# FFN output projection of a hybrid transformer block: one product of float32 operands in place of three products of split parts

## The chip, the cores and the metric

The kernel runs on one core of a Trainium2 chip. The core has a matrix engine (TensorE, PE in the profile, with its loads of stationary operands listed apart as PEld), a vector engine (VectorE, DVE), a scalar engine (ScalarE, ACT), a general engine (GpSimd, POOL) and an engine that here issues most of the DMAs (SyncE, SP). Each engine works through its own queue of instructions in order and waits on semaphores for the others. The matrix engine takes a stationary operand (`lhsT`) and a moving operand (`rhs`) from SBUF and adds the product into a PSUM bank.

The metric is the time of one execution on the device in microseconds, as the median of several runs. A profile is one further execution with the hardware profiler on.

## The reference

The whole block has a mixer of three branches and then a feed-forward network. Only its last lines matter here: 512 tokens, `D_MODEL` 1024, `D_FF` 2816, everything in float32.

```python
    h = rms_norm(x, ffn_pre_g[l])
    gate, up = jnp.split(h @ w_ffn_in[l], 2, axis=-1)
    x = x + rms_norm((jax.nn.silu(gate) * up) @ w_ffn_out[l], ffn_post_g[l])
```

The changed product is `(silu(gate) * up) @ w_ffn_out`, a 512 x 2816 matrix times a 2816 x 1024 matrix.

## The kernel before

**The two kinds of operand.** The program marks a matrix operand either as plain `F32` or as `F32R`, which is four bytes in memory too. Where a dense product matters for accuracy, the kernel splits a float32 value `v` into two `F32R` parts: a high part `h`, written by ScalarE in a copy that rounds, and a low part `l = v - h`, written by VectorE. A product of two split operands is then three matrix instructions, high by high, high by low, low by high, added in the same PSUM bank. `mm3` issues them, and all the large projections of the kernel go through it. Its three instructions have lines 137, 138 and 139 in the profile:

```python
        first = mm(ps, lhsT=lh, rhs=rh, start=start, stop=False)
        mm(ps, lhsT=lh, rhs=rl, start=False, stop=False)
        return first, mm(ps, lhsT=ll, rhs=rh, start=False, stop=stop)
```

Smaller products elsewhere in the kernel take plain `F32` operands directly: in the attention heads line 1138 multiplies the transposed probabilities by the values (80 calls in the source: 8 heads of 1 + 2 + 3 + 4 tiles, each a 128 x 128 by 128 x 128 product), line 1001 multiplies squares by a column of ones, and line 843 forms 32 x 32 blocks of scores.

**Weights.** `slab` brings a piece of a weight matrix of 128 x 512 values (256 KB) from HBM into a staging tile `wsD` of the pool `wD`, splits it into `whD` and `wlD`, and returns both. Each of the three names has three buffers in rotation (`bufs=3`), unless the caller wants the split parts kept in a pool of its own:

```python
        st = self.t(self.wd, [P, m, n], "wsD", bufs=3)
        nc.sync.dma_start(st, src)
        h, l = (self.t(pool or self.wd, [P, m, n], t, F32R, hold or 3) for t in ("whD", "wlD"))
        nc.scalar.copy(h, st)
        self.split_low(l, st, h)
```

The DMA is issued by SP (line 201), the copy by ScalarE (line 205), the subtraction by VectorE (line 132, in `split_low`).

**The feed-forward network.** `ffn` first runs over the 22 row blocks of `w_ffn_in` in pairs (`stream`, at the PSUM tiles `mmD`). For each block, `up` multiplies gate and up part (line 1261), and then writes the result `t` halved and split: `fH` by ScalarE (line 1262) and `fL` by VectorE (line 1263). `fH` and `fL` are tiles of 128 x 22 x 512 values, 44 KB of each partition apiece, and live in the pool `ffn` with the buffers of the output projection.

Then `project` multiplies by `w_ffn_out`. It is also used once earlier, for `w_out` after the three branches, with the split operands `mH` and `mL`. The 1024 output columns are done in two halves (`n`), each with four PSUM banks `po0` to `po3`, one for each 128 tokens. Within a half the loop goes over the 22 blocks `k` of the contraction: one slab of weights, and for each of the four token tiles one product, 128 tokens of `x` as the stationary operand and the slab's 512 columns as the moving one (`part`). The second half does so for the first 16 slabs only; the last 6 (`hold`) are kept in the pool `ffn`, and the token tiles are finished one after the other over these six, so that the norm of one tile runs beside the products of the next. Behind each tile's last product come a sum of squares on ScalarE (line 1232), a multiplication by the gain on VectorE (line 1233), in the second half the reciprocal root on GpSimd (line 279), the addition to the residual (line 1286) and the store (line 1287). The residual `x1` is read back from HBM (line 1281) into tiles that held the FFN's input before.

**Order.** The program is written with a tile framework that inserts the waits. It orders instructions by a priority that rises along the program; `lane` moves parts of the program to other priorities, and `lane(0)` puts the weight splits ahead. A buffer of a rotating tile is given to its next user when its last reader is done.

Of the kernel before, what the change touches and what calls it, by code (L numbers as in the profile page):

```python
# [11 lines left out]
F32 = mybir.dt.float32  # L12
F32R = mybir.dt.float32r
# [3 lines left out]
AF = mybir.ActivationFunctionType  # L17
ALU = mybir.AluOpType
# [4 lines left out]
P = 128  # L23
S = 512
# [10 lines left out]
KF = DFF // P  # L35
# [67 lines left out]
class Kern:  # L103
# [92 lines left out]
    def slab(self, src, pool=None, hold=None):  # L196

        nc = self.nc
        m, n = src.shape[1:]
# [3 lines that stand above are left out]
        cur = self.cur_lane  # L203
        self.lane(0)
        nc.scalar.copy(h, st)  # L205
        self.split_low(l, st, h)
        self.lane(cur)
        return h, l
# [996 lines left out]
    def project(self, pool, pp, x, w, nk, gp, done, hold):  # L1205


        nc = self.nc
        V, A = nc.vector, nc.scalar
        w = w.rearrange("(k p) n -> p k n", p=P)  # L1210
        y = [self.t(pool, [P, D], f"y{i}") for i in range(NT)]
        ss = self.t(pool, [P, NT, 2], "pss")
        for n in range(2):
            c = slice(n * 512, (n + 1) * 512)
            ps = [self.t(pp, [P, 512], f"po{i}") for i in range(NT)]

            def part(i, k, wk):
                h, l = wk
                tok = slice(i * P, (i + 1) * P)
                self.mm3(ps[i], x[0][:, k, tok], x[1][:, k, tok], h[:, 0], l[:, 0], k == 0, k == nk - 1)  # L1220

            first = nk - hold * n
            for k in range(first):
                wk = self.slab(w[:, k:k + 1, c])
                for i in range(NT):
                    part(i, k, wk)
            held = [self.slab(w[:, k:k + 1, c], pool, hold) for k in range(first, nk)]
            for i in range(NT):
                for k in range(first, nk):
                    part(i, k, held[k - first])  # L1230
                junk = self.t(pool, [P, 512], "pjk", bufs=2)
                A.activation(junk, ps[i], AF.Square, accum_out=ss[:, i, n:n + 1])
                V.tensor_tensor(y[i][:, c], ps[i], gp[:, c], op=ALU.mult)
                if n:
                    s1, tm, rs = (self.t(pool, [P, 1], t, bufs=2) for t in ("rs1", "rtm", "rrs"))
                    V.tensor_tensor(s1, ss[:, i, 0:1], ss[:, i, 1:2], op=ALU.add)
                    self.rstd(rs, s1, D, NEPS, tm)
                    done(i, y[i], rs)

    def ffn(self, x1d):  # L1240
        nc, tc, ins = self.nc, self.tc, self.ins
        V, A = nc.vector, nc.scalar
        es = self.ctx
        fp = es.enter_context(tc.tile_pool(name="ffn", bufs=1))
        fH, fL = self.t(fp, [P, KF, S], "fH", F32R), self.t(fp, [P, KF, S], "fL", F32R)
        gp = self.t(fp, [P, D], "gp")
        nc.scalar.dma_start(gp, ins["ffn_post_g"][0:1, :].to_broadcast([P, D]))
        win = ins["w_ffn_in"][0].rearrange("(k p) n -> p k n", p=P)
        self.stream_psum(es, 4)
        po = es.enter_context(tc.tile_pool(name="pfo", bufs=1, space=PSUM))  # L1250
        for f in range(0, KF, 2):
            ts_ = [self.t(fp, [P, S], f"ft{j}", bufs=2) for j in range(2)]

            def gate(j, pg):
                t = ts_[j]
                A.activation(t, pg, AF.Tanh, scale=0.5)
                V.scalar_tensor_tensor(t, t, 1.0, pg, op0=ALU.add, op1=ALU.mult)

            def up(j, pu):
                t = ts_[j]  # L1260
                V.tensor_tensor(t, t, pu, op=ALU.mult)
                A.activation(fH[:, f + j], t, AF.Copy, scale=0.5)
                V.scalar_tensor_tensor(fL[:, f + j], t, 0.5, fH[:, f + j].bitcast(F32), op0=ALU.mult, op1=ALU.subtract)

            wg, wu = win[:, :, f * P:(f + 2) * P], win[:, :, DFF + f * P:DFF + (f + 2) * P]
            if f:
                self.stream(wg, self.h, gate)
                self.stream(wu, self.h, up)
            else:

                a, b = slice(0, S // 2), slice(S // 2, S)
                pg = self.stream(wg, self.h, None, a)
                pu = self.stream(wu, self.h, None, a)
                self.stream(wg, self.h, gate, b, pg)
                self.stream(wu, self.h, up, b, pu)


        x1 = [[self.t(self.hp, [P, 512], f"xH{2 * i + n}") for n in range(2)] for i in range(NT)]
        for i in range(NT):
            for n in range(2):  # L1280
                nc.sync.dma_start(x1[i][n], x1d[i][:, n * 512:(n + 1) * 512])

        def done(i, y, rs):
            for n in range(2):
                c = slice(n * 512, (n + 1) * 512)
                V.scalar_tensor_tensor(x1[i][n], y[:, c], rs, x1[i][n], op0=ALU.mult, op1=ALU.add)
                nc.sync.dma_start(self.out[0, i * P:(i + 1) * P, c], x1[i][n])

        self.project(fp, po, (fH, fL), ins["w_ffn_out"][0], KF, gp, done, 6)

    def run(self):
        self.full = True
# [73 lines left out]
```

## Time and profile before

| What | Value |
|---|---|
| median of 2 runs | 1406.16 us (1403.6 to 1408.73) |
| the profiled execution, on the same clock as the runs | 1408.42 us |
| its span, first to last instruction | 1406.6 us |
| mean granted TensorE clock | 0.996 of full speed |
| VectorE busy | 848.3 us (60%), 1756 instructions |
| ScalarE busy | 638.6 us (45%), 1259 instructions |
| HBM read and written | 169.65 MB and 60.16 MB |

A row of a group or tile gives the line in the program, the engine, the operation, the tiles as `out<-in`, the shape, the number of instructions and their durations. For a matrix instruction `128*128 128x512` means 128 contraction rows by 128 stationary columns, with 512 moving columns. The profile writes `f32` for matrix operands of either kind. Matrix instructions overlap: a duration of 389 ns says that one instruction is in the engine for so long, while the next starts much sooner, so the cost in a row of them is the distance between starts. Durations of waiting instructions are not in the busy time, but idle time before an instruction is listed with what ended it.

### The profile page before, as it was taken

The page shows a single profiled execution, that of the slowest core. Times are in us where ns is not written, and L with a number is a line of the kernel's source. Part 1 is how long each engine was busy: PE and PEld are TensorE (multiplying, and loading weights), DVE is VectorE, ACT ScalarE, POOL GpSimd, SP SyncE. Part 2 cuts the span into 40 slices and gives each one's busy share as a digit, 9 for nine tenths or more (in the row PEclk, how much of TensorE's full clock was granted, in tenths as well). Part 3 has the DMA queues.
Part 4 walks back from the last instruction along what each step waited for, and adds up shares of the span by engine and source line. Part 5 has one row for each costly group of instructions (what it writes and reads, how often), then busy time and mean ns, then how long its engine had stood idle before and what let it go on. Part 6 is the DMA issues. An engine that isn't in the chain of part 4 may idle for free.

```text
span 1406.6 us, 27356 instructions
## 1 busy us (share of the span) xinstructions
PE 1354.8 (96%) x9664; PEld 1103.2 (78%) x9664; DVE 848.3 (60%) x1756; ACT 638.6 (45%) x1259; POOL 190.8 (14%) x1042
## 2 busy tenths in 40 slices
PE   6999999999999999999999999999999999999998
PEld 5777777777777777888788888877888888888886
DVE  5567797797787784575665576655575344343234
ACT  5554546556556453433665354443354333332222
POOL 2122132131222311242210000001010000000000
PEclk9999999999999999999999999999999999999999
DMA  5565467557755777986464555415544333334233
GB/s 180 149 193 144 129 183 227 178 153 218 213 157 155 242 237 227 356 277 208 137 204 147 157 178 168 130 53 173 198 139 135 98 97 92 102 95 156 97 98 105
DMA packets 196025, 231.62 MB, mean 165 GB/s; under 512 B 42672, under 2 KB 137392, under 8 KB 195888
## 3 DMA queue, kind: packets, MB, share of 16 engines
q1 hardware_dynamic: 194496, 226.72, 52.1%
q10 hardware_dynamic: 1392, 3.15, 0.7%
q8 instruction: 76, 1.25, 0.4%
q14 instruction: 61, 0.50, 0.1%
HBM read 169.65 MB, written 60.16 MB: 163 GB/s over the span
## 4 chain that ended last, share of the span: by engine, by line
PE 82%; DMA 6%; DVE 4%; issue 4%; ACT 3%; POOL 1%; SPq 1%; POOLq 0%; DVEq 0%; ACTq 0%
PE mmD L137 18%; PE mmD L138 17%; PE mmD L139 17%; PE po L137 4%; PE po L139 4%; PE po L138 4%; PE pr L194 1%; DMA wsD<-in_w_in_dram 1%; DMA z<-zst 1%; DMA zr<-z 1%; PE pmo L1138 1%; PE pm L137 1%; PE pm L139 1%; PE pm L138 1%; PE ph L843 1%
## 5 line engine op out<-in xcount | busy, mean ns | idle before, releaser
L137 PE MATMUL mmD<-xH,whD 128*128 128x512 f32 (+1 forms) x1232 | 486.2, 397 | 11.9 <-POOL token L149 5.6
L138 PE MATMUL mmD<-xL,whD 128*128 128x512 f32 (+1 forms) x1232 | 474.2, 386 | 0.0
L139 PE MATMUL mmD<-xH,wlD 128*128 128x512 f32 (+1 forms) x1232 | 469.6, 385 | 0.9 <-DVE wlD L132 0.9
L132 DVE TENSOR_TENSOR wlD<-wsD,whD 128x512 fp32r<-128x512 f32 x384 | 263.2, 687 | 292.0 <-ACT whD L205 276.0
L205 ACT CAST whD<-wsD 128x512 fp32r<-128x512 f32 x384 | 236.7, 618 | 375.8 <-PE mmD L138 244.1
L137 PEld LDWEIGHTS mmD<-xH,whD 128*128 128x128 f32 x1232 | 232.0, 189 | 65.2 <-POOL token L149 8.9
L139 PEld LDWEIGHTS mmD<-xH,wlD 128*128 128x128 f32 x1232 | 232.2, 189 | 48.6 <-DVE wlD L132 2.0
L138 PEld LDWEIGHTS mmD<-xL,whD 128*128 128x128 f32 x1232 | 233.5, 190 | 40.1
L149 POOL MEMSET token<- 1x1 f32 x912 | 82.2, 90 | 675.4 <-PE mmD L139 660.1
L139 PE MATMUL po<-whD,fL 128*128 128x512 f32 x176 | 68.6, 390 | 0.0
L138 PE MATMUL po<-wlD,fH 128*128 128x512 f32 x176 | 68.6, 390 | 0.0
L137 PE MATMUL po<-whD,fH 128*128 128x512 f32 x176 | 61.9, 390 | 0.0
L279 POOL TENSOR_TENSOR rrs<-rtm,mhalf 128x1 f32<-128x1 f32 x8 | 4.4, 551 | 402.3 <-DVE rtm L274 368.7
L646 DVE TENSOR_TENSOR invtmp<-inv 64x30 f32<-64x30 f32 (+14 forms) x120 | 38.7, 322 | 17.7 <-DMA inv<-Ld 16.0
L594 POOL TENSOR_SCALAR BK<-BK,gC 128x128 f32<-128x128 f32 x56 | 47.0, 854 | 11.8 <-PE pr L194 11.8
L237 ACT COPY zst<-mmD 128x512 f32<-128x512 f32 x64 | 37.3, 583 | 14.6 <-PE mmD L139 14.4
L647 DVE TENSOR_TENSOR inv<-inv,invtmp 64x30 f32<-64x30 f32 (+14 forms) x120 | 38.4, 320 | 2.2
L139 PEld LDWEIGHTS po<-whD,fL 128*128 128x128 f32 x176 | 33.0, 188 | 7.0
L138 PEld LDWEIGHTS po<-wlD,fH 128*128 128x128 f32 x176 | 33.0, 188 | 7.0
L137 PEld LDWEIGHTS po<-whD,fH 128*128 128x128 f32 x176 | 33.0, 188 | 7.0
L843 PEld LDWEIGHTS ph<-hq,hk 128*32 128x32 f32 x1536 | 17.6, 111 | 18.0 <-issue 9.6
L1136 ACT COPY mpT<-pmt 128x128 f32<-128x128 f32 (+3 forms) x32 | 13.6, 425 | 38.0 <-PE pmt L1134 37.9
(349 smaller groups left out, 1960.1 us busy)
## 6 DMA issues: line engine op xcount, KB each, us to landing
wsD<-in_w_in_dram SPq DMA_DIRECT2D x176, 256.0 KB, 3.4
wsD<-in_w_ffn_in_dram SPq DMA_DIRECT2D x96, 256.0 KB, 2.8
z<-zst SPq DMA_DIRECT2D x63, 256.0 KB, 3.3
rwd<-G SPq DMA_DIRECT2D x28, 512.0 KB, 5.5
G<-rwd SPq DMA_DIRECT2D x28, 512.0 KB, 6.7
wsD<-in_w_branch_dram SPq DMA_DIRECT2D x48, 256.0 KB, 2.9
wsD<-in_w_ffn_out_dram SPq DMA_DIRECT2D x44, 256.0 KB, 2.6
zr<-z SPq DMA_DIRECT2D x26, 256.0 KB, 3.3
```

The costliest lines, as they stand in the source:

```text
L132: (eng or self.nc.vector).tensor_tensor(dst, src, high.bitcast(F32), op=ALU.subtract)
L137: first = mm(ps, lhsT=lh, rhs=rh, start=start, stop=False)
L138: mm(ps, lhsT=lh, rhs=rl, start=False, stop=False)
L139: return first, mm(ps, lhsT=ll, rhs=rh, start=False, stop=stop)
L149: token = self.nc.gpsimd.memset(self.token, 0.0).ins
L194: last = c()
L205: nc.scalar.copy(h, st)
L237: self.nc.scalar.copy(st[:m], ps)
L594: Pl.tensor_scalar(BK[:, c], BK[:, c], gC[:, c + 1:c + 2], None, op0=ALU.mult)
L646: V.tensor_tensor(tv, cv, rv, op=ALU.mult)
L647: V.tensor_tensor(U[:, :j, j + 1:], U[:, :j, j + 1:], tv, op=ALU.add)
L843: mm(g[b:b + HB, o // P, :], lhsT=k[:, t], rhs=q[:, t], start=True, stop=True)
```

## The change

The values that `up` writes are kept as one plain float32 tile `fx`; the VectorE instruction for the low part is gone. `project` takes either a pair (as `w_out` still passes) or one tile. For one tile, `part` issues one plain float32 product instead of `mm3`, and a local `slab` only loads the weights: there is no copy, no subtraction, and no split tiles. The plain weights lie in the staging tile `wsD` itself, three buffers in rotation in `wD` for the streamed slabs, six in the pool `ffn` for the held ones.

```diff
@@ project
+        plain = not isinstance(x, tuple)
...
             def part(i, k, wk):
+                tok = slice(i * P, (i + 1) * P)
+                if plain:
+                    nc.tensor.matmul(ps[i], lhsT=x[:, k, tok], rhs=wk[:, 0], start=k == 0, stop=k == nk - 1)
+                    return
                 h, l = wk
-                tok = slice(i * P, (i + 1) * P)
                 self.mm3(ps[i], x[0][:, k, tok], x[1][:, k, tok], h[:, 0], l[:, 0], k == 0, k == nk - 1)
+
+            def slab(k, own=None, hold=3):
+                if not plain:
+                    return self.slab(w[:, k:k + 1, c], own, hold)
+                st = self.t(own or self.wd, [P, 1, 512], "wsD", bufs=hold)
+                nc.sync.dma_start(st, w[:, k:k + 1, c])
+                return st
 
             first = nk - hold * n
             for k in range(first):
-                wk = self.slab(w[:, k:k + 1, c])
+                wk = slab(k)
                 for i in range(NT):
                     part(i, k, wk)
-            held = [self.slab(w[:, k:k + 1, c], pool, hold) for k in range(first, nk)]
+            held = [slab(k, pool, hold) for k in range(first, nk)]
@@ ffn
-        fH, fL = self.t(fp, [P, KF, S], "fH", F32R), self.t(fp, [P, KF, S], "fL", F32R)
+        fx = self.t(fp, [P, KF, S], "fx")
...
                 V.tensor_tensor(t, t, pu, op=ALU.mult)
-                A.activation(fH[:, f + j], t, AF.Copy, scale=0.5)
-                V.scalar_tensor_tensor(fL[:, f + j], t, 0.5, fH[:, f + j].bitcast(F32), op0=ALU.mult, op1=ALU.subtract)
+                A.activation(fx[:, f + j], t, AF.Copy, scale=0.5)
...
-        self.project(fp, po, (fH, fL), ins["w_ffn_out"][0], KF, gp, done, 6)
+        self.project(fp, po, fx, ins["w_ffn_out"][0], KF, gp, done, 6)
```

## The prediction

> **What bounds the kernel now.** I read the page's busy times first, then the busy times by stage, then the tile `po`, then the waits. The page says that the matrix engine is nearly always at work:
>
> ```profile
> PE 1354.8 (96%) x9664; PEld 1103.2 (78%) x9664; DVE 848.3 (60%) x1756; ACT 638.6 (45%) x1259; POOL 190.8 (14%) x1042
> ```
>
> An average over stages with different limits proves nothing for the one that changes, so the second view cuts out the end of the kernel: the FFN input projection, the two halves of the output projection, and the tail behind it.
>
> ```profile
> core 0: us, PE busy (x) PEld busy (x) DVE busy (x) ACT busy (x) POOL busy (x), PEclk, DMA share, GB/s
> 1040.00:1279.30 239.30, 239.30 (x1145) 201.91 (x1145) 108.78 (x167) 85.91 (x146) 0.00 (x0) 1.00 0.39 112
> 1279.30:1341.50 62.20, 62.20 (x276) 51.50 (x275) 20.12 (x30) 17.45 (x33) 0.00 (x0) 1.00 0.32 107
> 1341.50:1399.40 57.90, 57.90 (x255) 47.37 (x253) 20.11 (x34) 13.90 (x25) 1.65 (x3) 1.00 0.29 96
> 1399.40:1406.60 7.20, 0.21 (x1) 0.00 (x0) 2.33 (x5) 0.69 (x2) 0.55 (x1) 0.87 0.38 146
> ```
>
> The output projection is the two middle rows: 62.2 + 57.9 = 120.1 us, in which PE has no idle time, while VectorE and ScalarE are busy for a third or less, at full granted clock (1.00) and a DMA share of about 0.3. Its matrix instructions are these:
>
> ```profile
> L137 PE MATMUL po<-whD,fH x176: 389/389/399, 1279.3 to 1398.7; 128*128 128x512 f32 x176
> L138 PE MATMUL po<-wlD,fH x176: 389/389/397, 1279.5 to 1399.0; 128*128 128x512 f32 x176
> L139 PE MATMUL po<-whD,fL x176: 389/389/397, 1279.7 to 1399.2; 128*128 128x512 f32 x176
> ```
>
> There are 3 x 176 = 528 of them, 2 halves x 22 blocks x 4 token tiles x 3. Each shows 389 ns, but the cost in a row is 120.1 / 528 = 227.5 ns from start to start. A product of split parts thus costs 682 ns. The other engines wait for PE here, not PE for them:
>
> ```profile
> ACT whD L205 <- PE po L139: 66.4, 31, 5.6
> ACT pjk L1232 <- PE po L139: 15.6, 5, 4.8
> ```
>
> So in this stage the time is the number of matrix instructions times their distance, and the change replaces both factors.
>
> **The change part by part.**
>
> *How many instructions.* The plain product is written as one call, but the trace shows what a plain float32 call becomes. Line 1138 is called 80 times in the source, and its row has twice that:
>
> ```profile
> L1138 PE MATMUL pmo<-mpT,mv x160: 270/275/377, 796.9 to 948.7; 128*128 128x128 f32 x160
> L1001 PE MATMUL pm<-ones,msq x40: 164/250/271, 668.2 to 680.7; 128*128 128x1 f32 x40
> L843 PE MATMUL ph<-hq,hk x1536: 189/196/218, 120.2 to 630.4; 128*32 128x32 f32 x192
> L1119 PE MATMUL pm<-ul,uh x32: 221/330/398, 786.2 to 941.1; 128*128 128x128 f32 x8, 128*128 128x256 f32 x8, 128*128 128x384 f32 x8, 128*128 128x512 f32 x8
> ```
>
> Line 1001 (20 calls, 40 instructions) agrees. So the stage will have 2 x 176 = 352 matrix instructions, not 176 and not 528.
>
> *What one of them costs.* No plain product in the trace has 512 moving columns, so the price is extrapolated. I take the minima of the rows above, since a minimum is an instruction whose stationary operand was already loaded. Plain passes: 164 ns with 1 column, 189 with 32, 270 with 128. That is (189 - 164) / 31 = 0.81 and (270 - 189) / 96 = 0.84 ns for a further column: a straight line, 0.835 from end to end. Split parts (`F32R`): 221 ns with 128 columns (line 1119) and 389 with 512 (`po`), (389 - 221) / 384 = 0.4375 ns a column. A plain pass costs 1.9 times as much for a column. The starts, which do not depend on how an end is modelled, say the same:
>
> ```profile
> 786.21 0.22 PE L1119 MATMUL pm<-ul,uh 128*128 128x128 f32 x1
> 786.27 0.27 PE L1120 MATMUL pm<-uh,ul 128*128 128x128 f32 x1
> ...
> 942.93 0.38 PE L1138 MATMUL pmo<-mpT,mv 128*128 128x128 f32 x2
> 943.15 0.38 PE L1134 MATMUL pmt<-cst,mp 128*128 128x128 f32 x2
> ```
>
> One pass of split parts over 128 columns gives way after 0.06 us; two plain passes over 128 columns after 0.22, or 0.11 each.
>
> With 512 columns a plain pass then lasts 164 + 511 x 0.835 = 591 ns, 202 more than the 389 of today, and its distance to the next is 227.5 + 202 = 429.5 ns; I take 430. Bounds from rows: from below 227.5, a split pass over the same columns; from above 4 x 0.11 us = 440 if all of a 128-column pass, the load of the stationary operand included, grew with the columns, and twice today's distance, 455, as the far end. I take the straight line, since three rows lie on it.
>
> *The sum.* 352 x 0.430 = 151.4 us instead of 120.1: +31.3 us. A product goes from 682 to 860 ns. Fewer instructions, but slower ones.
>
> The Trainium skill ("FP8 and Floating Point Precision", section "TensorE Precision Notes") has true FP32 as four passes through the array (high by high, high by low, low by high, low by low), against one pass for the reduced form. By that, and with the trace's 227.5 ns for each pass, a product would cost 910 ns (an estimate) and the sum would be +40.1 instead of +31.3. The rows above agree in kind, two instructions of almost double price, and stay somewhat below it in size.
>
> *The work taken from VectorE and ScalarE.* The splits in the stage and the low parts in the FFN input stage go away:
>
> ```profile
> L132 DVE TENSOR_TENSOR wlD<-wsD,whD 128x512 fp32r<-128x512 f32 x42 | 29.0, 692 | 70.0 <-ACT whD L205 70.0
> L205 ACT CAST whD<-wsD 128x512 fp32r<-128x512 f32 x42 | 26.2, 623 | 73.2 <-PE po L139 66.4 <-DMA wsD<-in_w_ffn_out_dram 6.7
> L1263 DVE SCALAR_TENSOR_TENSOR fL<-ft,fH x22: 682/685/689, 1064.0 to 1281.3; 128x512 fp32r<-128x512 f32 x22
> ```
>
> That is 44 x 0.69 + 22 x 0.685 = 45 us of VectorE and 44 x 0.62 = 27 us of ScalarE. I count none of it: in the windows above PE is busy throughout, so this work lies beside it. If PE were waiting for it, that would show as idle time, and there is none between 1040 and 1399.4.
>
> *The loads.* Same number, same size. What moves is the moment at which a buffer comes free. Before, a `wsD` buffer was free once it was split; now it is free only after the four products that read it. With three buffers, a slab's load can start when the slab three places ahead is done, so it has two slabs of PE work, 2 x 4 x 0.86 = 6.9 us, to be issued and to land.
>
> ```profile
> wsD<-in_w_ffn_out_dram SPq DMA_DIRECT2D x44, 256.0 KB, 2.6
> ...
> 1267.03 3.06 SPq L201 DMA_DIRECT2D wsD<-in_w_ffn_out_dram  x2
> ...
> 1281.41 97.68 SPq L201 DMA_DIRECT2D wsD<-in_w_ffn_out_dram  x39
> ```
>
> It lands in 2.6 us (median), so some 4 us are to spare: cost nothing. If a load took longer than 6.9 us, PE would stand for the difference at each of up to 35 streamed slabs (22 + 16, less the first three). At the start, the first slabs are issued from 1267.03 on, into buffers freed by splits of the FFN input stage, which do not change; PE wants them at 1279.3. On SP, a waiting slab load now has behind it the next slab loads only, and at the end the stores, which come after all loads. The six held slabs have buffers of their own and can be loaded any time before; 1.5 MB more in flight during the FFN input stage meet a DMA share of 0.39. Nothing.
>
> *The turn and the tail.* Between the halves a bank must be read by lines 1232 and 1233 before it is written anew:
>
> ```profile
> L1233 DVE TENSOR_TENSOR y<-po,gp 128x512 f32<-128x512 f32 x7 | 4.6, 687 | 7.2 <-ACT pjk L1232 7.2
> ...
> L1232 ACT ACTIVATE pjk<-po 128x512 f32<-128x512 f32 x7 | 4.2, 596 | 12.1 <-PE po L139 12.1
> ```
> The two readers take 0.6 and 0.69 us, and PE works on the three other token tiles meanwhile, 3 x 0.68 = 2.0 us now and 2.6 then, so there is no new wait. The tail behind the last product (7.2 us in the last window) does the same work. The residual's loads and the first half's `fx` blocks are there long before they are used.
>
> *Memory.* `fL` and the low parts of the held slabs leave the pool `ffn`, so its tiles move to other addresses and may wait for other earlier tiles. What could be affected is the start of the FFN input stage, where PE waits for the norm anyway. I take nothing, with 1 us either way.
>
> Against the profiled execution (1408.4 us, 2.3 above the median of the runs) this gives 1439.7; against the median, 1406.2 + 31.3 = 1437.5 us.
>
> **The rivals.**
>
> *Not slower: a pass over 512 columns costs the same as now.* If a long plain pass ran at one split pass's distance, 352 x 0.2275 = 80.1 us, -40.0, or 1366 us. It decides the sign at 120.1 / 352 = 341 ns a pass: below that the change gains. For it: the plain rows end at 128 columns, and a part of their price could be loading the stationary operand (medians of 275 and 250 ns show such waits). Against it: the minima of three rows lie on one line, and the load of 128 columns is the same in the 1-column row, which has 164 ns.
>
> *A plain instruction costs twice a split one.* If the array took every moving column twice at today's full distance, an instruction would cost 2 x 227.5 = 455 ns and the stage 160.2 us: +40.1, 1446 us. For it: two plain passes over 128 columns take 0.22 us, one split pass 0.06, not far from four times. Against it: by the column the ratio is 0.835 to 0.4375, 1.9, and what is fixed in the distance is paid once. The rule of four passes of the Trainium skill ("FP8 and Floating Point Precision", "TensorE Precision Notes") would give this case.
>
> *Within 2%.* 2% of 1406.2 is 28.1 us, about what a measurement of this kernel can tell from no change. It is undercut with a pass of (120.1 + 28.1) / 352 = 421 ns, 2% less than my 430, or with a side gain of 3.2 us. Where could that come from? From the FFN input stage, if its 239.3 us shrank by 1.3% with fewer VectorE accesses to the same memory. Nothing in the rows says so. With 4.5 us from there it would be 1433 us.
>
> *The loads come late.* If a slab took 8 us instead of 2.6, PE would lose 1.1 us x 35 = 39 us more, 1476. Against it: the median, and that PE reads no more bytes a microsecond than before.
>
> **How the numbers follow.** My forecast (423 to 437 ns a pass, 1435 to 1440 us) 0.77, the double price 0.07, loads late 0.04, side gain or a cheaper pass 0.08, a pass at today's distance 0.03, the rest is unnamed. The range of 8 in 10 is 1431 to 1447: from a pass of 411 ns or side gains of 6 us up to the double price; it leaves out the late loads, the pass at today's distance and half of the side gains. Since +31.3 us is only 2.2%, a part of my own forecast, 0.12, comes out within 2%; with the side gains that is 0.21. Faster 0.03. Slower 0.76: 0.65 of the forecast, the double price and the late loads.
>
> **What would show it.** In the changed profile: the tile `po` with 352 plain instructions in the FFN stage, about 591 ns each, and starts 0.43 us apart; PE still busy without gaps from 1279 to about 1431; no casts or subtractions in that stretch; slab loads landing in under 7 us; the same 7.2 us behind. I am wrong if the distance is below 421 ns, if PE waits for `wsD`, or if the stage does not begin within a microsecond or two of 1279.3.

## The result, and the profile after

The changed kernel took 1445.47 us (median of 2 runs, 1442.77 to 1448.18) beside 1406.16 us before: a ratio of 1.0275, with a 95% interval of 1.0237 to 1.0313. It is slower. Measured again later, with four runs of it beside nine of the kernel before (median 1406.1), the median was 1438.94 us and the ratio 1.0235 (1.0215 to 1.0255). The profiled execution took 1448.18 us, its span is 1446.4 us, and the 39.8 us more than before come from these places.

The busy times of the changed kernel, a row for each stretch: the FFN input projection up to a gap, the gap, the 5 us behind it, the rest of the input projection, the output projection, and the tail. `PEclk` is the granted TensorE clock as a share of full speed.

```profile
core 0: us, PE busy (x) PEld busy (x) DVE busy (x) ACT busy (x) POOL busy (x), PEclk, DMA share, GB/s
1057.00:1064.00 7.00, 7.00 (x61) 7.00 (x59) 3.81 (x8) 3.32 (x6) 0.00 (x0) 1.00 0.88 261
1064.00:1068.00 4.00, 0.43 (x4) 0.22 (x2) 1.27 (x2) 0.63 (x2) 0.00 (x0) 0.79 0.92 329
1068.00:1073.00 5.00, 4.96 (x12) 3.90 (x13) 2.08 (x3) 2.18 (x4) 0.00 (x0) 0.50 0.44 121
1073.00:1288.20 215.20, 215.20 (x951) 178.32 (x950) 78.43 (x116) 69.78 (x116) 0.00 (x0) 1.00 0.36 103
1288.20:1439.20 151.00, 151.00 (x353) 66.77 (x351) 10.43 (x20) 5.59 (x16) 1.65 (x3) 1.00 0.23 74
1439.20:1446.40 7.20, 0.18 (x1) 0.00 (x0) 2.32 (x5) 0.69 (x2) 0.55 (x1) 0.68 0.26 100
```

The output projection takes 151.0 us instead of 120.1, again with PE busy throughout and the clock at 1.00. VectorE is down to 10.4 us of work in it and ScalarE to 5.6; nothing is gained by that. The tail is 7.2 us as before. The tile `po` gives the price of one instruction:

```profile
L1222 PE MATMUL po<-wsD,fx x352: 590/592/593, 1288.2 to 1438.8; 128*128 128x512 f32 x176
```

352 plain instructions of 592 ns each, and 151.0 / 352 = 429 ns from start to start.

The other rows hold what was not foreseen: in the third row PE has 0.43 us of work in 4 us, and in the fourth it starts 12 instructions in 5 us at half the granted clock. To cut the time at the same events in both kernels, I take the last transpose of the FFN's norm (tile `tr`) as the beginning of the input projection, first before, then after:

```profile
L357 PE MATMUL tr<-cst,xn x64: 270/272/475, 7.3 to 1054.4; 128*128 128x128 f32 x64
```

```profile
L357 PE MATMUL tr<-cst,xn x64: 269/273/477, 7.1 to 1057.0; 128*128 128x128 f32 x64
```

| Stretch | before, us | after, us | difference |
|---|---|---|---|
| start to last transpose | 1054.4 | 1057.0 | +2.6 |
| last transpose to first output product | 224.9 (to 1279.3) | 231.2 (to 1288.2) | +6.3 |
| output projection | 120.1 | 151.0 | +30.9 |
| tail | 7.2 | 7.2 | 0.0 |

The first difference lies ahead of all the change touches. In the ten profiles of this study, of kernels that are alike up to there, that transpose starts anywhere from 1047.0 to 1057.0, and the changed kernel itself has it at 1052.8 in its second profile. The second difference is the gap, and the timeline of PE shows it (start, duration, engine, line, instruction, and in brackets the idle time before it and what ended it):

```profile
1064.15 0.28 PE L139 MATMUL mmD<-xH,wlD 128*128 128x256 f32 x1
1068.04 0.79 PE L137 MATMUL mmD<-xH,whD 128*128 128x512 f32 x1 [3.62 <-ACT whD L205]
1068.63 0.63 PE L138 MATMUL mmD<-xL,whD 128*128 128x512 f32 x1
1069.06 0.63 PE L137 MATMUL mmD<-xH,whD 128*128 128x512 f32 x1
```

PE stands for 3.6 us for a high part of an input weight, and then the instructions start some 430 ns apart where 227 is usual. The view of waits between 1060 and 1070 says what the high part waits for (engine, line, releaser: total, count, longest):

```profile
ACT whD L205 <- DMA wsD<-in_w_ffn_in_dram: 5.9, 1, 5.9
...
PE mmD L137 <- ACT whD L205: 3.6, 1, 3.6
```

A load of `w_ffn_in` lands late. SP's own timeline shows what stands ahead of it: start, duration of the group, and how many DMAs it issued. First before, then after.

```profile
1038.47 226.25 SPq L201 DMA_DIRECT2D wsD<-in_w_ffn_in_dram  x90
```

```profile
1041.09 15.95 SPq L201 DMA_DIRECT2D wsD<-in_w_ffn_in_dram  x10
1057.31 1.77 SPq L1231 DMA_DIRECT2D wsD<-in_w_ffn_out_dram  x4
1059.18 1.40 SPq L201 DMA_DIRECT2D wsD<-in_w_ffn_in_dram  x2
1060.63 3.10 SPq L1231 DMA_DIRECT2D wsD<-in_w_ffn_out_dram  x2
1063.83 209.76 SPq L201 DMA_DIRECT2D wsD<-in_w_ffn_in_dram  x78
```

Before, SP issued 90 input loads without another between them. After, the six held slabs of `w_ffn_out` (line 1231), wanted some 360 us later (38 slabs of 4 x 0.858 us into the output projection), stand between the tenth, the twelfth and the thirteenth. The cast waits for the first load behind four of them, the eleventh, issued at 1059.18. It is not issued late: it goes out 2.2 us behind the start of the last transpose, as the same load did before (1056.55, after 1054.4). But it takes 8.1 us to land instead of 3.7, and the cast starts at 1067.37. The last figure of these rows is the time from issue to landing, before and then after:

```profile
wsD<-in_w_ffn_in_dram SPq DMA_DIRECT2D x1, 256.0 KB, 3.7
```

```profile
wsD<-in_w_ffn_in_dram SPq DMA_DIRECT2D x1, 256.0 KB, 8.1
```

So its data come late, in a stretch with a DMA share of 0.92; the experiments below test whether the held loads ahead of it are the reason. The last held load also waits on SP; what it holds up is the thirteenth input load, which is not the one that PE waits for:

```profile
SPq L1231 <- DMA gp<-in_ffn_post_g_dram: 2.0, 1, 2.0
```

The theory to test was therefore: the price of a plain instruction makes some 31 us, and the early held loads some 5 more, in the stretch ahead of the output projection. Its rivals: that the price belongs to something that came with the change (other buffers, other addresses, the splits gone), that the three split instructions would be as slow if they were two, and that the gap is chance.

### The profile page after: what moved, and what is told of

Its sections match the earlier page's. It is cut to its first block, busy times and chain, and to the rows that moved or that the text cites. A ratio compares the mean times of both kernels' runs of the same rounds, so it can differ in the third digit from the quotient of the medians.

```text
span 1446.4 us, 26836 instructions
## 1 busy us (share of the span) xinstructions
PE 1390.2 (96%) x9488; PEld 1075.0 (74%) x9488; DVE 805.2 (56%) x1690; ACT 611.0 (42%) x1215; POOL 190.9 (13%) x1042
## 4 chain that ended last, share of the span: by engine, by line
PE 80%; DMA 6%; DVE 5%; issue 4%; ACT 3%; SPq 1%; POOL 1%; POOLq 0%; ACTq 0%; DVEq 0%
PE mmD L137 17%; PE mmD L138 16%; PE mmD L139 16%; PE po L1222 10%; DMA wsD<-in_w_in_dram 1%; PE pr L194 1%; PE pmo L1138 1%; PE pm L137 1%; PE pm L139 1%; PE pm L138 1%; DMA z<-zst 1%; PE po L138 1%; PE po L137 1%; PE po L139 1%; PE ph L843 1%
## 5 line engine op out<-in xcount | busy, mean ns | idle before, releaser
L132 DVE TENSOR_TENSOR wlD<-wsD,whD 128x512 fp32r<-128x512 f32 x340 | 232.8, 686 | 234.4 <-ACT whD L205 216.7
L205 ACT CAST whD<-wsD 128x512 fp32r<-128x512 f32 x340 | 209.2, 618 | 302.7 <-PE mmD L138 243.5
L1222 PE MATMUL po<-wsD,fx 128*128 128x512 f32 x352 | 151.2, 592 | 0.0
L1222 PEld LDWEIGHTS po<-wsD,fx 128*128 128x128 f32 x352 | 67.0, 190 | 83.7 <-issue 83.6
L1245 DVE TENSOR_TENSOR y<-po,gp 128x512 f32<-128x512 f32 x16 | 11.0, 690 | 141.7 <-ACT pjk L1244 141.7
L1244 ACT ACTIVATE pjk<-po 128x512 f32<-128x512 f32 x16 | 9.5, 597 | 150.7 <-PE po L1222 145.0
L843 PE MATMUL ph<-hq,hk 128*32 128x32 f32 x1536 | 24.0, 201 | 3.1 <-DVE hk L868 2.6
L1138 PEld LDWEIGHTS pmo<-mpT,mv 128*128 128x128 f32 x160 | 22.5, 191 | 4.9 <-ACT mpT L1136 2.6
```

Of the source, the lines that this page charges most:

```text
L132: (eng or self.nc.vector).tensor_tensor(dst, src, high.bitcast(F32), op=ALU.subtract)
L843: mm(g[b:b + HB, o // P, :], lhsT=k[:, t], rhs=q[:, t], start=True, stop=True)
L1222: nc.tensor.matmul(ps[i], lhsT=x[:, k, tok], rhs=wk[:, 0], start=k == 0, stop=k == nk - 1)
```

## The experiments

Spans vary in the part ahead of the change, so each profile is cut as above: "stretch" is the time from the last transpose to the first output product, "stage" the output projection. "Landing" is the time that the first input load behind that transpose takes from issue to landing; it goes out 2.2 us behind the transpose in every kernel (2.5 with twelve slabs held), and the kernel before had 3.7 us, the first profile after 8.1. The kernels ran in two groups of four, each beside nine runs of the kernel before, with a median of 1406.1 us in the first group and 1404.29 us in the second.

| Kernel | stretch, us | landing, us | stage, us | median, us (runs) | ratio (95% interval) |
|---|---|---|---|---|---|
| first group: changed kernel again | 229.9 | 7.6 | 151.1 | 1438.94 (4) | 1.0235 (1.0215 to 1.0255) |
| held slabs loaded late | 225.0 | 4.1 | 151.8 | 1438.23 (5) | 1.0222 (1.0203 to 1.0241) |
| plain product alone | 225.6 | 4.9 | 151.0 | 1436.64 (4) | 1.0215 (1.02 to 1.0229) |
| held slabs from POOL's queue | 227.3 | 5.9 | 151.1 | 1441.21 (4) | 1.025 (1.0236 to 1.0264) |
| second group: products of 256 columns | 228.4 | 7.7 | 151.9 | 1436.3 (1) | |
| two split products | 225.0 | 4.0 | 80.7 | 1367.58 (4) | 0.9726 (0.9701 to 0.9752) |
| twelve slabs held | 230.0 | 7.5 | 151.1 | 1440.31 (4) | 1.0246 (1.0218 to 1.0274) |
| held slabs loaded one by one | 224.9 | 4.1 | 151.1 | 1435.29 (5) | 1.0211 (1.018 to 1.0241) |

### The changed kernel again

No edit; it says whether the gap comes back.

> The changed kernel once more, to size the part outside the product. Theory A (the six held slabs' loads, now issued ahead of the FFN input stage's own loads, make PE stand near 1064 us): the gap of about 3.7 us between line 139 and line 137 is there again, the stretch of lower granted clock behind it too, and the ratio is again 1.025 to 1.028. Theory B (that gap was a late transfer of one execution): no gap over 1 us there, the output projection 151.0 us as in the first profile, and the ratio near (1406.2 + 31) / 1406.2 = 1.022.

It came back. In the windows around it PE has 0.89 us of work in 4 us, and then a granted clock of 0.66 (columns as above):

```profile
1060.00:1064.00 4.00, 0.89 (x6) 0.60 (x5) 1.76 (x3) 1.30 (x3) 0.00 (x0) 1.00 0.91 323
1064.00:1069.00 5.00, 5.00 (x17) 3.91 (x16) 2.12 (x4) 2.13 (x4) 0.00 (x0) 0.66 0.55 158
```

The stretch is 229.9 us (from 1052.8 to 1282.7), 5.0 more than before, and the stage 151.1. On SP four held loads and then two more stand among the input loads, as in the first profile, with 1059.25 as the time of the first input load behind all six. The ratio is 1.0235, less than the 1.025 to 1.028 that was expected with the gap and more than the 1.022 without it. The profiled execution is the longest of the four (1442.78 us); two others took 1437.04 and 1436.58 us. As the part ahead varies by several microseconds, times without a profile don't tell in how many of them PE stood.

### The plain product alone

The kernel before with all its splits, buffers and loads. Only the three products of the FFN output projection become one plain product, of the high parts; both low parts are left out of it, though they are still computed.

```diff
             def part(i, k, wk):
...
+                if nk == KF:
+                    nc.tensor.matmul(ps[i], lhsT=x[0][:, k, tok].bitcast(F32), rhs=h[:, 0].bitcast(F32),
+                                     start=k == 0, stop=k == nk - 1)
+                    return
```

> The kernel before with one thing changed: in the FFN output projection one plain float32 product of the high parts instead of the three split ones. The low parts are still computed and loaded, but are left out of this product. Theory (the price is the plain pass alone): 352 instructions at 429 ns, the stage 151.0 us instead of 120.1, no gap near 1064 us, ratio 1.022. Rival (the price or part of it comes with the operands that lie in the staging buffers, or the freed VectorE and ScalarE work gave something back): the stage differs from 151 us by more than 1 us.

Its tile `po`, and the busy times of its output projection:

```profile
L1221 PE MATMUL po<-whD,fH x352: 590/592/593, 1276.7 to 1427.3; 128*128 128x512 f32 x176
```

```profile
1276.70:1427.70 151.00, 151.00 (x353) 66.67 (x351) 40.25 (x64) 31.05 (x58) 1.65 (x3) 1.00 0.24 83
```

The stage takes 151.0 us, as in the changed kernel, with 40.3 us of VectorE work and 31.1 us of ScalarE work still in it. So the price belongs to the plain product and to nothing else in the change, and the work taken off the two engines bought nothing. There is no gap, only one wait of PE of 0.4 us: the stretch is 225.6 us. This kernel isolates the product at 1406.1 + 30.5 us.

### Products of 256 columns

The changed kernel with each plain product cut into two halves of the moving columns.

```diff
-                    nc.tensor.matmul(ps[i], lhsT=x[:, k, tok], rhs=wk[:, 0], start=k == 0, stop=k == nk - 1)
+                    for o in (slice(0, 256), slice(256, 512)):
+                        nc.tensor.matmul(ps[i][:, o], lhsT=x[:, k, tok], rhs=wk[:, 0, o],
+                                         start=k == 0 and not o.start, stop=k == nk - 1 and bool(o.start))
```

> The changed kernel with each plain product cut into two of 256 moving columns: 704 instructions of half the width. If the price goes by the columns, as the straight line of the prediction has it, the distance is 215 to 218 ns and the stage 151 to 153 us. If a good part of it were fixed for each instruction, as the loading of the stationary operand, the stage would grow by 100 ns or more for each of 352 added instructions, to 186 us or above.

```profile
L1223 PE MATMUL po<-wsD,fx x704: 377/379/379, 1275.4 to 1427.1; 128*128 128x256 f32 x176
```

Twice the instructions, and the stage is 151.9 us, 0.9 more: 215.8 ns apart instead of 429. The price goes by the columns, and almost nothing is paid for an instruction as such. In duration, 164 + 255 x 0.835 = 377 ns by the prediction's line for 256 columns, and the row shows 377 to 379. The distances, which don't depend on how an end is modelled, say the same: 429 / 512 and 215.8 / 256 are both 0.84 ns a column. Why a plain column takes nearly twice the time of a split one is not shown by any run.

### Two split products

The kernel before, with high by high and low by high only: 352 instructions, as many as after the change. The low part of the weights is left out of the product.

```diff
+                if nk == KF:
+                    nc.tensor.matmul(ps[i], lhsT=x[0][:, k, tok], rhs=h[:, 0], start=k == 0, stop=False)
+                    nc.tensor.matmul(ps[i], lhsT=x[1][:, k, tok], rhs=h[:, 0], start=False, stop=k == nk - 1)
+                    return
```

> The kernel before with two split products in the FFN output projection, high and low part of the activations by the high part of the weights; the low part of the weights is computed but left out of the product. As many instructions as the changed kernel has, 352. Theory (the change lost because a plain instruction costs 429 ns, not because of their number): 352 x 0.2275 = 80 us, the stage 40 us shorter than before, 1366 us, ratio 0.972. Rival (with 1.82 us of PE work a slab the loads and splits bind, some 4.7 us in three buffers, or 1.6 us a slab, are near): idle time in the stage, 1370 us or more.

The busy times of its output projection, and then its tail:

```profile
1276.20:1356.90 80.70, 80.47 (x353) 65.69 (x351) 36.06 (x59) 30.73 (x58) 1.07 (x2) 1.00 0.42 139
1356.90:1366.10 9.20, 0.17 (x1) 0.00 (x0) 5.37 (x11) 0.69 (x2) 1.47 (x2) 0.71 0.60 228
```

The stage falls to 80.7 us, 229 ns an instruction, of which PE is idle for 0.2 us, so the loads and splits don't bind here, though the rival expected it. 2.0 us are lost again in the tail, where VectorE has 5.4 us of work instead of 2.3. With the same number of instructions as the changed kernel the stage is 70 us shorter; the loss is the price of one, not their number. The kernel as a whole takes 0.9726 of the time before (0.9701 to 0.9752). It is faster than both, but it computes a product without the weights' low part.

### The held slabs loaded late

The changed kernel, in which the loads of the six held slabs wait for the first product of the output projection.

```diff
+                    m = nc.tensor.matmul(ps[i], lhsT=x[:, k, tok], rhs=wk[:, 0], start=k == 0, stop=k == nk - 1)
+                    self.first_plain = self.first_plain or m
...
+                d = nc.sync.dma_start(st, w[:, k:k + 1, c])
+                if own is not None:
+                    self.tc.add_manual_dep(d.ins, self.first_plain.ins.name, mybir.DependencyInfo(
+                        mybir.DependencyClass.Sync, mybir.DependencyReason.DATA), reason="late")
```

> The held slabs' loads wait for the first product of the output projection, so they cannot run ahead. Theory A: the gap near 1064 us and the lower clock behind it are gone, the output projection still takes 151 us, and the time is 5 to 6 us below that of the changed kernel beside it, near 1437 us or a ratio of 1.022. Theory B: the time is that of the changed kernel beside it, within 1.5 us.

The gap is gone from the place where it was (a window at the same distance from the last transpose):

```profile
1060.00:1064.00 4.00, 4.00 (x20) 3.32 (x19) 3.09 (x5) 3.02 (x5) 0.00 (x0) 1.00 0.46 137
```

The stretch is 225.0 us (1052.8 to 1277.8). The six loads now go out together as the output projection begins, ahead of the streamed slabs on SP, and there PE stands for 0.5 us:

```profile
1288.73 1.55 PE L1223 MATMUL po<-wsD,fx 128*128 128x512 f32 x3 [0.52 <-DMA wsD<-in_w_ffn_out_dram]
```

The stage shows it with 151.8 us instead of 151.1. A part of the gap moved with the loads. The input load now lands in 4.1 us instead of the 7.6 of the profile above, issued at the same 1055.01 in both. In time the forecast missed: 5 to 6 us less than the changed kernel beside it were expected, and the medians differ by 0.7. That the gap is gone rests on the trace.

### The held slabs loaded one by one

The same, with each held load waiting for the last product of another slab of the second half: load j for slab 2j.

```diff
+                    m = nc.tensor.matmul(ps[i], lhsT=x[:, k, tok], rhs=wk[:, 0], start=k == 0, stop=k == nk - 1)
+                    self.last_of[k] = m
...
+                    self.tc.add_manual_dep(d.ins, self.last_of[2 * (k - nk + 6)].ins.name, mybir.DependencyInfo(
+                        mybir.DependencyClass.Sync, mybir.DependencyReason.DATA), reason="late")
```

> The changed kernel with each of the six held loads behind a product of the second half, one for every second slab. Neither the gap near 1060 us nor the 0.7 us that PE stood with all six loads in one place at the start of the projection: stage 151.0 us, from the last transpose to the first product of the stage 225 us as before the change, ratio 1.020 to 1.022 (1434 to 1437 us).

Both stretches, the input projection and the output projection, in its busy times:

```profile
1055.60:1280.50 224.90, 224.90 (x1023) 187.50 (x1022) 85.40 (x128) 76.11 (x127) 0.00 (x0) 1.00 0.36 108
1280.50:1431.60 151.10, 151.10 (x353) 66.69 (x351) 10.43 (x20) 5.67 (x16) 1.65 (x3) 1.00 0.25 84
```

No idle time of PE in either: 224.9 us, the value of the kernel before, and 151.1 us. In the trace the loss of 5 us is undone wholly. In the medians it is not told apart. Against their own kernel before, the changed kernel is 32.8 us slower, with late held loads 32.1, with spread ones 31.0, and the intervals of the three ratios overlap. The plain product alone, also without the gap, is 30.5 us slower. So the medians put the held loads at 0.7 to 2.3 us, less than the 4.3 to 5.0 us by which the stretches of their single profiles differ.

### The held slabs from POOL's queue

The changed kernel with the held loads issued by GpSimd, so that SP's order is that of before.

```diff
-                nc.sync.dma_start(st, w[:, k:k + 1, c])
+                (nc.gpsimd if own is not None else nc.sync).dma_start(st, w[:, k:k + 1, c])
```

> The changed kernel with the six held loads issued by GpSimd instead of SP. If the gap near 1064 us comes from the order on SP (held loads, and a wait of one of them, ahead of the input stage's loads), SP is free and the gap is under 1 us, ratio near 1.022. If it comes from the bytes in flight (1.5 MB more at the same time), the gap stays at 2 us or more and the ratio near 1.026.

```profile
1060.00:1064.00 4.00, 2.62 (x13) 2.03 (x13) 1.89 (x3) 0.62 (x1) 0.00 (x0) 1.00 1.02 370
1064.00:1069.00 5.00, 4.53 (x21) 3.42 (x20) 1.99 (x3) 2.93 (x6) 0.00 (x0) 1.00 0.37 109
```

PE stands for 1.4 and 0.5 us and the clock stays at 1.00. The stretch is 227.3 us, 2.4 over the 224.9 of before, instead of 5.0 over it. So with SP's order restored about half of the loss stays. The input load lands in 5.9 us, between the 4.1 with late held loads and the 7.6 of the changed kernel. The DMA share in the first window is 1.02, against 0.46 in the same window with late held loads: the bytes of the held slabs are in flight beside those that PE wants. Neither of the two forecasts held as it stood, and the division between bytes and order is not settled, since the held loads also went out at other times: from POOL all six between 1053.79 and 1057.25, from SP four by 1054.91 and the last at 1058.81. The median doesn't show a gain over the changed kernel.

### Twelve slabs held

The changed kernel with 12 held slabs instead of 6.

```diff
-        self.project(fp, po, fx, ins["w_ffn_out"][0], KF, gp, done, 6)
+        self.project(fp, po, fx, ins["w_ffn_out"][0], KF, gp, done, 12)
```

> The changed kernel with 12 held slabs instead of 6, so twice as many loads ahead of the input stage's. If loads ahead are what makes PE stand near 1060 us, the gap there grows from 3.4 to 3.7 us by 3 to 6 us and the time lies 3 to 6 us above the changed kernel (1442 to 1445, ratio 1.025 to 1.028). If the gap has another cause, it stays below 4 us and the time at 1439.

```profile
1052.46 2.01 SPq L1231 DMA_DIRECT2D wsD<-in_w_ffn_out_dram  x4
1054.57 1.16 SPq L201 DMA_DIRECT2D wsD<-in_w_ffn_in_dram  x2
1055.78 3.56 SPq L1231 DMA_DIRECT2D wsD<-in_w_ffn_out_dram  x3
1059.44 0.38 SPq L201 DMA_DIRECT2D wsD<-in_w_ffn_in_dram  x1
1060.62 3.20 SPq L1231 DMA_DIRECT2D wsD<-in_w_ffn_out_dram  x5
```

The busy times in the gap and in the 5 us behind it:

```profile
1059.00:1063.00 4.00, 0.76 (x6) 0.56 (x6) 1.49 (x3) 0.85 (x2) 0.00 (x0) 1.00 1.07 383
1063.00:1068.00 5.00, 5.00 (x16) 3.95 (x17) 1.88 (x3) 1.96 (x4) 0.00 (x0) 0.66 1.06 372
```

This missed: the gap did not grow (3.2 us of idle time, stretch 230.0 us). Twice the bytes cost nothing more, though the DMA share stayed at 1.06 in the 5 us after the gap too. The input load that PE waits for is the one at 1054.57, and as in the changed kernel only four held loads stand ahead of it; it lands in 7.5 us, against 7.6 there. The other eight held loads come behind it. That the loads ahead of the first missing one decide, and not their total, fits both the row and the time; a number between none and four was not tried.

## Why the prediction was right, and where it wasn't

The prediction was 1437.5 us within 1431 to 1447, slower. The first two runs gave 1445.47, the four later ones 1438.94. That 1445.47 still lies in the range is partly luck: its upper end was put there for the double price of an instruction, which did not come, and the held loads and the part ahead of the change took that room. The 1.4 us between 1437.5 and 1438.94 say little too, since the part ahead varies by several microseconds.

*How many instructions, and what one costs.* 352 instructions of 592 ns at a distance of 429 ns, where 591 and 430 were forecast; the stage is 151.0 us against 151.4. The straight line through three rows of other widths held four times beyond its last point, and the products of 256 columns lie on it too. The plain product alone gave the same 151.0 us, so this term is shown to be the cause, not only to agree in size.

*The four passes.* By the trace a plain product of 512 columns takes 2 x 429 = 858 ns, which is 3.77 times the 227.5 ns of a split pass. The rule of four passes of the Trainium skill ("FP8 and Floating Point Precision", "TensorE Precision Notes") is near it, and its estimate of 910 ns is 6% too high here. The page states no number of passes for the reduced form, and no run shows how many an instruction makes; in this trace a split product's calls are one instruction each, 176 for 176. The rival that the estimate stood beside, 160.2 us for the stage, is refuted by 151.0.

*The work taken from VectorE and ScalarE* was counted as nothing, and was nothing: the stage is as long with it as without.

*The streamed slabs, the turn, the tail, memory.* Nothing, as said. The streamed slabs land in 2.7 us (median), PE has no idle time in the stage, and the tail is 7.2 us again. What the moved addresses do to the start can't be told from the 2.6 us ahead of the change, which vary between executions.

*The held slabs: the step that failed.* "The six held slabs have buffers of their own and can be loaded any time before; 1.5 MB more in flight during the FFN input stage meet a DMA share of 0.39. Nothing." The first half was right and was the trouble: because they can be loaded at any time, they were issued as soon as their memory was free, in a place where the input projection has little to spare. The share of 0.39 was an average from 1040 to 1279.3. Around the start of the projection the kernel before already had this:

```profile
1055.00:1059.00 4.00, 4.00 (x35) 4.00 (x35) 2.94 (x5) 2.98 (x6) 0.00 (x0) 1.00 0.85 268
```

The sentence about SP, that a waiting slab load has only the next slab loads behind it, took the queue in the order of the output projection and did not ask what a load without a wait is moved ahead of. The first input load behind four of them landed in 8.1 us instead of 3.7, and PE stood for it. It cost 6.3 us in the first profile and 5.0 in the second. Moved behind the start of the projection, the loads cost 0.7 us in its stage, and spread out none; these are spans of single profiles, which the medians bear out in sign but don't separate.

*The sum.* Against the profiled execution 1439.7 us were forecast and 1448.18 came, 8.5 more: 6.3 from the held loads, 2.6 from the part ahead of the change, which differs between executions, and 0.4 less in the stage. The condition named for being wrong, that the output projection does not begin within a microsecond or two of 1279.3, is where it showed (1288.2). As a sign it was too narrow: in the four other kernels without a gap that start lies anywhere from 1276.2 to 1280.5.

*The other rivals.* A pass at today's distance (80.1 us) is refuted by 151.0; it is what two split products cost (80.7). A side gain in the input projection is refuted by 224.9 us in the kernel with spread loads: equal, with 13 us less of VectorE work in that stretch (98.8 us before, 85.4 there), as this row of the kernel before says:

```profile
1054.40:1279.30 224.90, 224.90 (x1024) 187.51 (x1022) 98.77 (x150) 77.38 (x129) 0.00 (x0) 1.00 0.38 109
```

Late loads inside the output projection did not occur; the mechanism did, one stage earlier.

## What to carry to other kernels

Before products are merged, price one instruction of the new kind by its columns, from rows of several widths: here 352 instead of 528 instructions made the stage 26% longer, and in a stage that PE fills, the work saved on other engines is worth nothing. A load that loses its dependency does not stay where it was: look up what it will stand ahead of on its queue, and take the DMA share of that moment rather than of the stage. A load issued in time can still land late behind it: 8.1 us here instead of 3.7.

## What the runs showed of the hardware

After it had stood for 3.6 us PE ran at a granted clock of 0.50 in the next 5 us; after 3.1 us (the changed kernel again) and 3.2 us (twelve held slabs) at 0.66. After 3.2 us in the kernel with 256 columns it stayed at 1.00:

```profile
1054.00:1058.00 4.00, 0.83 (x6) 0.58 (x5) 1.69 (x3) 1.07 (x3) 0.00 (x0) 1.00 0.92 325
1058.00:1063.00 5.00, 5.00 (x24) 4.09 (x23) 2.35 (x4) 2.37 (x5) 0.00 (x0) 1.00 0.54 142
```

After the 1.4 us of the POOL queue's kernel it stayed at 1.00 too. The 0.66 is a mean over the window. In windows of 0.1 us the clock in these places is either 0.50 or 1.00, and it was 0.50 for 6.8 us in the first profile (from 1066.35), for 3.4 us in the changed kernel again (from 1064.46) and for 3.4 us with twelve held slabs (from 1063.57). In the second of these:

```profile
1064.50:1067.80 3.30, 3.30 (x10) 2.52 (x9) 1.28 (x2) 1.24 (x3) 0.00 (x0) 0.50 0.55 161
```

At 0.50 instructions start some 430 ns apart instead of 227, so about half of the time in which PE works is lost. With the idle time this makes 3.6 + 2.6 of the 6.3 us in the first profile, 3.1 + 1.7 of 5.0 in the second and 3.2 + 1.7 of 5.1 with twelve slabs; the kernel with 256 columns, at full clock, lost 3.5 with 3.2 of idle time. So a short wait can cost half as much again, or more, in clock.

The Trainium skill ("TensorE: Matmul & The Clock Gate", "Part 1: The HAM clock gate") has a half rate after an idle window of about 3.4 us that runs freely, so that the same gap may or may not fill one. The lengths of the low stretches, 3.4 us and twice that, and the two outcomes after 3.2 us agree with a window of that size. That PE must be idle for the whole of one does not: in the first profile the clock fell at 1066.35, 1.9 us after PE had stopped, and in the two others 1.1 and 0.7 us after PE had started again. That a free-running window is the reason was not tried here.
